# A transformer layer in fp32 split matmuls: single third and fourth tiles at the beginning, modulation passes three steps behind their request, and one multiply moved into the last wait

## The chip, the cores and the metric

The kernel runs on one core of a Trainium2 chip. The metric is the device time of one execution in microseconds. The page of the profile shows one execution, taken with the hardware profiler, on the engines PE (matrix multiply), DVE (vector), ACT (scalar), POOL and SP; PEld is the loading of weights into PE, and SP mostly issues DMA requests.

## The reference

The reference is one layer of a diffusion transformer, followed by a final RMSNorm. There are 256 latent tokens and 256 context tokens, the model width is 2048 (16 tiles of 128), the hidden width of a feed-forward half is 5632 (44 tiles), and everything is float32.

```python
mod_l = (silu_c @ w_mod[l] + b_mod[l]).reshape(B, N_MOD, D_MODEL)      # nine vectors of 2048
mod_c = (silu_cc @ w_mod[l] + b_mod[l]).reshape(1, N_MOD, D_MODEL)
xl = half_step_ffn(xl, mod_l, 0, g_norm[l, 0], w_ffn1_up[l], w_ffn1_down[l])
xc = half_step_ffn(xc, mod_c, 0, g_norm[l, 0], w_ffn1_up[l], w_ffn1_down[l])
hl = adaln(xl, g_norm[l, 1], mod_l, 3)         # rms_norm(x, g) * (1 + mod[i + 1]) + mod[i]
hc = adaln(xc, g_norm[l, 1], mod_c, 3)
...                                            # projections, attention (8 heads), mLSTM (8 heads), w_out
xl = xl + mod_l[:, 5, None, :] * mixer_output(att_l, hm_l, m_l[3], m_gain[l], w_out[l])
xl = half_step_ffn(xl, mod_l, 6, g_norm[l, 2], w_ffn2_up[l], w_ffn2_down[l])
return rms_norm(xl, g_final)
```

A half step is `x + 0.5 * gate * ((silu(a) * b) @ w_down)` with `a, b` the two halves of `adaln(x) @ w_up`. The nine modulation vectors come from a product of one row (two, with the context's) with a matrix of 2048 x 18432.

## The kernel before

**Arithmetic.** Each float32 product is made of three matmuls on parts: a number is split into `hi` (rounded to PE's reduced float32, by ACT, line 128) and `lo` (the remainder, by DVE, line 129), and hi·hi, lo·hi and hi·lo are added in one PSUM bank (`mm3`, line 152). So each weight that arrives by DMA costs ACT one pass, DVE one pass, and PE three matmuls for each block of tokens.

**The beginning.** The first feed-forward needs modulation vectors 0 (shift, `SH`) and 1 (scale, `SC`), which come from the first 32 transfers of 1 MB, `in_w_m`, into four buffers `mraw`. `BLOCKS` says in which order d-model tiles are made ready: tiles 0 and 1 singly, then pairs. For a single tile one transfer gives its shift and one its scale, and `mod_sums` makes both on PE (16 matmuls each, `tr<-mraw,cP`). For a pair four transfers are needed: the shift of its first tile is made by DVE (two passes over the transfer, `junkv<-mraw,cB`, one for each of the two conditions), the shift of its second and the scales of both by PE (16 matmuls of 128 columns, 16 of 256). `mod_turned` then turns the sums into columns (`tr<-ident,row`), x is transposed (`tr<-ident,xs`), scaled, and split into `hhi` and `hlo`. The generator `products` multiplies the tiles that are ready with the first six blocks of columns of the up-projection (weights `raw<-in_w_pre`), in six banks, three matmuls per bank and tile: `mm<-hhi,hi`, `mm<-hhi,lo`, `mm<-hlo,hi`. It gives back control after each bank, and the caller puts one bank's matmuls between two groups of modulation sums, by `steps(prods, n)`. All of this is `Pinned`: PE, DVE and SP work it off in the order in which it is written. `idle(n)` puts n matmuls without a use on PE.

**The mixer.** Vectors 5 to 8 are needed later. Their weights, `in_w_mt`, come as halves of 512 KB into a few slots, and DVE makes one pass (line 208, 128x1024) over each. The class `Beside` hands these passes out: its generator `steps` is called once for each step of the main work, and starts the next pass when the table `PACE` says so and its slot was requested (the transfer is requested a step after the slot's last pass). A step is a weight tile of a projection. The passes' own order on DVE is fixed; between them and the other instructions a scheduler sets the order when the kernel is built. Slots `sr` serve the projections; while the attention and the output projection run, two slots `late` and one or more of `sr` are in use. There DVE also makes the softmax's maximum (line 1683), reciprocal (1688) and scaling (1689, `pr`), which PE transposes (line 1695), and the `lo` parts of `w_out`.

**The end.** `last2` makes the last block of the second feed-forward's down-projection for 256 columns at a time, adds it to the stream (`acc`), and applies the final norm. For the second half of the tokens the last 512 columns come in two halves: DVE adds the first half (line 2348), squares and sums it (2304), multiplies columns 1024 to 1535 by the final gains (`multiplied(1, 2)`, line 2300), adds the second half, squares it, and adds up the sums (2308). POOL makes the power -1/2 of that (2310), and DVE and ACT scale with it (2356, 2358, 2360) and store.

Of the kernel before, what the change touches and what calls it, by code (L numbers as in the profile page):

```python
# [9 lines left out]
F32 = mybir.dt.float32  # L10
# [9 lines left out]
P = 128  # L20
# [13 lines left out]
N_IDLE = 6, 4, 5, 2, 3  # L34
# [10 lines left out]
BLOCKS = ((0, 1), (1, 2)) + tuple((k, k + 2) for k in range(2, 16, 2))  # L45
# [13 lines left out]
def tile_layer(ctx: ExitStack, tc: tile.TileContext, I: dict, out: bass.AP):  # L59
# [207 lines left out]
    class Beside:  # L267
# [5 lines left out]
        def __init__(self, sp, i0, i1, tiles, pace):  # L273
            self.cB = sp.tile([P, 1024], F32, name="cBl", bufs=1)
            self.items = half_items(i0, i1)
            self.pace = pace
            self.slots = {}
# [129 lines left out]
    def products(n_ffn, pre, k0, k1, hhi, hlo, early=False, both=False, middle=False):  # L407
# [26 lines left out]
        for u0 in range(0, 2 * NPRE, most):  # L434
# [3 lines left out]
            if u0 + most < 2 * NPRE and not ahead:  # L438
                ahead.append(load(u0 + most))
            for u in range(nu):  # L440
# [6 lines left out]
                for k, (wh, wl) in ws:  # L447
                    tensor[0].matmul(b, wh, hlo[:, k, :], start=False, stop=k == KT - 1)  # L448
# [13 lines left out]
    with pool(name="st", bufs=1) as st:  # L462
        scratch.append(st)
        cP = st.tile([P, KT, 32], F32, name="cP")
        nc.gpsimd.memset(cP, 0.0)
        pc = tbank()
# [9 lines left out]
        sel = st.tile([96, P], BF16, name="sel")[:, :32]  # L476
        with nc.allow_low_precision("each sum has one term that is not zero, and that is one"):
            vector[0].tensor_reduce(sel, ident[:96, :96].rearrange("p (j q) -> p q j", j=3), axis=AX.X, op=ALU.add)
        c3 = tbank()[:96, :P]
        stack = st.tile([32, P], F32, name="stack")  # L480
        vector[0].tensor_copy(stack[:, :96].rearrange("p (j q) -> p j q", j=3), ident[:32, :32].unsqueeze(1).to_broadcast([32, 3, 32]))
# [78 lines left out]
        def mod_sums(i, k0, k1, last=iter(())):  # L560
# [75 lines left out]
        mod_turned()  # L636
        for s in (CTX, LAT):
            scale_of(0, s, slice(0, 1))
# [10 lines left out]
        for k0, k1 in BLOCKS[1:]:  # L649
            kk = slice(k0, k1)  # L650
            following = products(1, pre, k0, k1, hhi, hlo, middle=True)
            if k1 - k0 == 2:
                raw = mod_unit()
            for i in range(2):
                for _ in mod_sums(i, k0 if i else k1 - 1, k1, following if i else iter(())):
                    steps(prods, 3 - (k1 - k0))
# [7 lines left out]
            if k0 != 2:  # L664
                steps(following)
            mod_turned()
            if k0 != 2:
                steps(prods)
            for s in (CTX, LAT):
                scale_of(0, s, kk)  # L670
            if k0 == 2:
# [13 lines left out]
            if k0 == 2:  # L685
# [1241 lines left out]
    with f2x:  # L1927
# [346 lines left out]
        def last2():  # L2274
# [70 lines left out]
            for h in range(2):  # L2345
# [113 lines left out]
```

## Time and profile before

| | us |
|---|---|
| three runs | 2594.56, 2595.95, 2599.84 (median 2595.95) |
| the profiled execution | 2596.07, of which its span is 2594.4 |
| PE busy | 2565.9 (99%) |
| DVE busy | 2183.9 (84%) |
| ACT busy | 1432.4 (55%) |
| DMA | mean 264 GB/s; 396 GB/s in the first fortieth of the span |

A number on a row of the timeline is the start in microseconds, then the duration, the engine, the line, the operation, output and inputs, shapes, and how often it stands there in a row; in square brackets stands how long the engine had been idle before it, and what ended that. In a table of windows each row is a stretch of time, with the busy microseconds of PE, PEld, DVE, ACT and POOL, each with its count of instructions, then the granted clock of PE (1.00 is full), the share of time in which the DMA engines were busy, and GB/s. PE is busy nearly throughout, so that a change shows in the time only where PE waits (28.5 us in all, 2594.4 less 2565.9), or where its work grows or shrinks.

### The profile page before, as it was taken

The page shows a single profiled execution, that of the slowest core. Times are in us where ns is not written, and L with a number is a line of the kernel's source. Part 1 is how long each engine was busy: PE and PEld are TensorE (multiplying, and loading weights), DVE is VectorE, ACT ScalarE, POOL GpSimd, SP SyncE. Part 2 cuts the span into 40 slices and gives each one's busy share as a digit, 9 for nine tenths or more (in the row PEclk, how much of TensorE's full clock was granted, in tenths as well). Part 3 has the DMA queues.
Part 4 walks back from the last instruction along what each step waited for, and adds up shares of the span by engine and source line. Part 5 has one row for each costly group of instructions (what it writes and reads, how often), then busy time and mean ns, then how long its engine had stood idle before and what let it go on. Part 6 is the DMA issues. An engine that isn't in the chain of part 4 may idle for free. (4 is left out here: it accounts for less than half of the span.)

```text
span 2594.4 us, 34281 instructions
## 1 busy us (share of the span) xinstructions
PE 2565.9 (99%) x12708; PEld 2141.1 (83%) x12708; DVE 2183.9 (84%) x2884; ACT 1432.4 (55%) x1838; POOL 220.5 (8%) x273
## 2 busy tenths in 40 slices
PE   7999999999999999999999999999999999999998
PEld 5788888888888888888889989888898888888887
DVE  6788888878888788888887899798889888888987
ACT  4454444544445565444454448456486676667764
POOL 0000000100000100000110000120000000001001
PEclk9999999999999999999999999999999999999999
DMA  9989999999999989889987897776768999999986
GB/s 396 353 215 266 267 287 273 259 275 287 257 291 264 279 245 244 213 220 224 230 255 258 294 328 239 239 282 212 261 229 251 274 275 277 283 280 284 272 247 174
DMA packets 127656, 684.73 MB, mean 264 GB/s; under 512 B 14200, under 2 KB 16760, under 8 KB 64896
## 3 DMA queue, kind: packets, MB, share of 16 engines
q1 hardware_dynamic: 98112, 490.63, 50.6%
q0 software_dynamic: 29376, 191.90, 37.5%
q8 instruction: 100, 1.64, 0.2%
q14 instruction: 68, 0.56, 0.1%
HBM read 664.59 MB, written 17.89 MB: 263 GB/s over the span
## 5 line engine op out<-in xcount | busy, mean ns | idle before, releaser
L128 ACT ACTIVATE hi<-raw 128x1024 fp32r<-128x1024 f32 (+2 forms) x488 | 505.6, 1040 | 412.6 <-PE mm L152 304.4
L129 DVE TENSOR_TENSOR lo<-raw,hi 128x1024 fp32r<-128x1024 f32 (+2 forms) x476 | 569.0, 1204 | 134.0 <-ACT hi L128 113.2
L128 ACT ACTIVATE hi<-chain 128x1024 fp32r<-128x1024 f32 x352 | 371.9, 1060 | 305.9 <-PE mm L152 184.4
L129 DVE TENSOR_TENSOR lo<-chain,hi 128x1024 fp32r<-128x1024 f32 x352 | 426.5, 1221 | 105.8 <-ACT hi L128 98.3
L152 PE MATMUL mm<-hi,hhi 128*128 128x512 f32 (+3 forms) x1024 | 394.0, 385 | 0.0
L152 PE MATMUL mm<-lo,hhi 128*128 128x512 f32 (+3 forms) x1024 | 386.9, 378 | 0.0
L152 PE MATMUL mm<-hi,hlo 128*128 128x512 f32 (+3 forms) x1024 | 386.4, 377 | 0.0
L208 DVE SCALAR_TENSOR_TENSOR junk<-sraw,cBh 128x1024 fp8e5<-128x1024 f32 x192 | 234.3, 1220 | 21.4 <-DMA sraw<-in_w_mt 19.0
L152 PEld LDWEIGHTS mm<-lo,hhi 128*128 128x128 f32 x1024 | 192.5, 188 | 33.8
L152 PEld LDWEIGHTS mm<-hi,hhi 128*128 128x128 f32 x1024 | 192.6, 188 | 31.1
L152 PEld LDWEIGHTS mm<-hi,hlo 128*128 128x128 f32 x1024 | 192.8, 188 | 30.7
L129 DVE TENSOR_TENSOR lo<-ra,hi 128x1024 fp32r<-128x1024 f32 x104 | 126.3, 1221 | 27.4 <-ACT hi L128 21.6
L128 ACT ACTIVATE hi<-ra 128x1024 fp32r<-128x1024 f32 x104 | 110.2, 1062 | 66.4 <-PE mm L152 40.5
L152 PE MATMUL mm<-lo,hid2h 128*128 128x512 f32 (+1 forms) x356 | 137.9, 387 | 0.1
L152 PE MATMUL mm<-hi,hid2h 128*128 128x512 f32 (+1 forms) x356 | 137.8, 387 | 0.0
L152 PE MATMUL mm<-hi,hid2l 128*128 128x512 f32 (+1 forms) x356 | 137.7, 387 | 0.0
L152 PE MATMUL mm<-hi,sumshl 128*128 128x512 f32 x400 | 123.2, 389 | 0.0
L730 POOL DMA_DIRECT2D chain<-in_w_up1b x60 | 53.1, 886 | 733.5 <-DVE lo L129 733.5
L208 DVE SCALAR_TENSOR_TENSOR sr<-sr,cBl 128x1024 f32<-128x1024 f32 x84 | 102.2, 1224 | 13.4 <-DMA sr<-in_w_mt 7.4
L152 PE MATMUL mm<-hi,sumshh 128*128 128x512 f32 x352 | 108.4, 389 | 0.0
L152 PE MATMUL mm<-hhi,hi 128*128 128x512 f32 (+1 forms) x288 | 101.3, 352 | 0.0
L152 PE MATMUL mm<-hhi,lo 128*128 128x512 f32 (+1 forms) x288 | 99.0, 344 | 0.0
(505 smaller groups left out, 5446.4 us busy)
## 6 DMA issues: line engine op xcount, KB each, us to landing
raw<-in_w_dn SPq DMA_DIRECT2D x70, 1024.0 KB, 9.7
chain<-in_w_up1b POOLq DMA_DIRECT2D x60, 1024.0 KB, 10.6
sraw<-in_w_mt SPq DMA_DIRECT2D x96, 512.0 KB, 8.1
sr<-in_w_mt SPq DMA_DIRECT2D x81, 512.0 KB, 5.6
raw<-in_w_up1b SPq DMA_DIRECT2D x40, 1024.0 KB, 8.0
mraw<-in_w_m SPq DMA_DIRECT2D x32, 1024.0 KB, 8.0
chain<-in_w_dn POOLq DMA_DIRECT2D x30, 1024.0 KB, 9.2
chain<-in_w_up2b POOLq DMA_DIRECT2D x28, 1024.0 KB, 11.2
```

Of the source, the lines that this page charges most:

```text
L128: scalar[0].activation(hi, src, AF.Copy)
L129: vector[0].tensor_tensor(lo, src, hi.bitcast(F32), op=ALU.subtract)
L152: tensor[0].matmul(out_ap, s, m, start=first and not n, stop=last and n == 2, skip_group_check=skip)
L208: ins = nc.vector.scalar_tensor_tensor(junk() if junk else raw, raw, 1.0, cB[s], op0=ALU.mult, op1=ALU.mult, accum_out=mT[:, i, s, kt, h : ...
L730: accum = lambda dst, src: nc.gpsimd.dma_start(dst, src, accum_op=ALU.add)
```

## The change

**The beginning.** `ALONE = 4`: tiles 2 and 3 become single tiles like 0 and 1, and pairs begin at tile 4. Tile 2's shift, which DVE made, is made by PE. A table `AHEAD` says how many banks of the preceding tile's products stand ahead of each group of sums. Four `idle` matmuls stand behind tile 0's turned rows. In single blocks the matmul with `hlo` comes one bank later than those with `hhi`. The transfer of the next products' weights is requested behind the request for modulation weights where it stood ahead of it. Two small tiles, `sel` and `stack`, are made earlier.

On PE, behind the products of the ones of `xs` (x transposed) and tile 0's two groups of sums, there stood (`mm<-hhi,hi` and its two companions are one bank's products; `tr<-mraw,cP` a unit of sums):

```order
L87 MATMUL tr<-mraw,cP 32x128 x16
L87 MATMUL tr<-ident,row 128x128 x2
L87 MATMUL tr<-mraw,cP 32x128 x16
L87 MATMUL mm<-hhi,hi 128x512
L87 MATMUL mm<-hhi,lo 128x512
L87 MATMUL mm<-hlo,hi 128x512
L87 MATMUL mm<-hhi,hi 128x512
L87 MATMUL mm<-hhi,lo 128x512
L87 MATMUL mm<-hlo,hi 128x512
L87 MATMUL tr<-mraw,cP 32x128 x16
```

And now, at the same place:

```order
L92 MATMUL tr<-mraw,cP 32x128 x16
L92 MATMUL tr<-ident,row 128x128 x2
L92 MATMUL mm<-ident 128x128 x4
L92 MATMUL mm<-hhi,hi 128x512
L92 MATMUL mm<-hhi,lo 128x512
L92 MATMUL mm<-hhi,hi 128x512
L92 MATMUL mm<-hhi,lo 128x512
L92 MATMUL mm<-hlo,hi 128x512
L92 MATMUL tr<-mraw,cP 32x128 x16
L92 MATMUL mm<-hhi,hi 128x512
```

Two banks of tile 0's products now come ahead of tile 1's first sums instead of behind them, and the first `hlo` matmul stands behind the second bank's first two. On SP, the order of requests was, from tile 1 on (`raw<-in_w_pre` are the weights of the products):

```order
L557 DMA mraw<-in_w_m 128x2048
L421 DMA raw<-in_w_pre 128x768
L557 DMA mraw<-in_w_m 128x2048 x4
L421 DMA raw<-in_w_pre 128x1536
L557 DMA mraw<-in_w_m 128x2048 x4
L421 DMA raw<-in_w_pre 128x1536
```

It is now:

```order
L566 DMA mraw<-in_w_m 128x2048 x2
L427 DMA raw<-in_w_pre 128x768
L566 DMA mraw<-in_w_m 128x2048 x2
L427 DMA raw<-in_w_pre 128x768
L566 DMA mraw<-in_w_m 128x2048 x2
L427 DMA raw<-in_w_pre 128x768
L566 DMA mraw<-in_w_m 128x2048 x4
L427 DMA raw<-in_w_pre 128x1536
```

The bytes are the same; tiles 2 and 3 have two smaller requests for their products' weights instead of one.

**The mixer.** `LEAD = 3`: a pass starts at the earliest three steps after its transfer was requested. On DVE, in the middle of the second half of the attention (`pr`, `sd` and `nm` belong to the softmax, `yo` and `x_` to the output projection), there stood:

```order
L1688 RECIPROCAL sd<-sd 128x1
L1823 TENSOR_TENSOR x_14449<-x_14449,yo 128x512
L1689 TENSOR_SCALAR pr<-pr,sd 128x512
L208 TENSOR_SCALAR late_14439,mT<-late_14439,cBl 128x1024
L1684 TENSOR_SCALAR nm<-nm 128x1
L129 TENSOR_TENSOR lo<-raw,hi 128x1024
L1688 RECIPROCAL sd<-sd 128x1
L208 TENSOR_SCALAR late_14439,mT<-late_14439,cBl 128x1024
L1689 TENSOR_SCALAR pr<-pr,sd 128x512
```

And now:

```order
L1702 RECIPROCAL sd<-sd 128x1
L1837 TENSOR_TENSOR x_14501<-x_14501,yo 128x512
L1703 TENSOR_SCALAR pr<-pr,sd 128x512
L213 TENSOR_SCALAR late_14492,mT<-late_14492,cBl 128x1024 x2
L213 TENSOR_SCALAR late_14493,mT<-late_14493,cBl 128x1024
L1697 TENSOR_REDUCE nm<-mm 128x1
L1836 TENSOR_TENSOR yo<-mm,gate 128x512
L1698 TENSOR_SCALAR nm<-nm 128x1
L134 TENSOR_TENSOR lo<-raw,hi 128x1024
L1702 RECIPROCAL sd<-sd 128x1
L1837 TENSOR_TENSOR x_14502<-x_14502,yo 128x512
L1703 TENSOR_SCALAR pr<-pr,sd 128x512
```

No pass stands between `sd` and `pr` now; three stand together behind a `pr`. Such a group of three `late` passes comes three times, and 12 passes instead of 8 follow the softmax's last `pr`.

**The end.** `multiplied(1, 2)` moves behind the last `factor`. DVE's last instructions were (`L2300` is the multiply):

```order
L2348 TENSOR_TENSOR acc_16127<-acc_16127,mm 128x256
L2304 TENSOR_SCALAR sab,rstd<-acc_16127 128x256
L2300 TENSOR_TENSOR acc_16127<-acc_16127,gf 128x512
L2348 TENSOR_TENSOR acc_16127<-acc_16127,mm 128x256
L2304 TENSOR_SCALAR sab,rstd<-acc_16127 128x256
L2308 TENSOR_REDUCE s_21134<-rstd 128x1
L2358 TENSOR_SCALAR acc_16127<-acc_16127,rstd 128x512
```

They are now:

```order
L2362 TENSOR_TENSOR acc_16185<-acc_16185,mm 128x256
L2318 TENSOR_SCALAR sab,rstd<-acc_16185 128x256
L2362 TENSOR_TENSOR acc_16185<-acc_16185,mm 128x256
L2318 TENSOR_SCALAR sab,rstd<-acc_16185 128x256
L2322 TENSOR_REDUCE s_21191<-rstd 128x1
L2314 TENSOR_TENSOR acc_16185<-acc_16185,gf 128x512
L2371 TENSOR_SCALAR acc_16185<-acc_16185,rstd 128x512
```

The multiply stands between the sum `s` and the scaling that waits for POOL.

The diff, cut to its core:

```diff
+LEAD = 3
-N_IDLE = 6, 4, 5, 2, 3
+N_IDLE = 6, 4, 5, 2, 3, 4
+AHEAD = {1: (2, 2, 1), 2: (0, 1, 2), 3: (0, 1, 2), 4: (1, 2, 2, 1)}
-BLOCKS = ((0, 1), (1, 2)) + tuple((k, k + 2) for k in range(2, 16, 2))
+ALONE = 4
+BLOCKS = tuple((k, k + 1) for k in range(ALONE)) + tuple((k, k + 2) for k in range(ALONE, 16, 2))
...
             pin(queue.dma_start(x, I["w_mt"][i - 2, kt, :, h * 1024 : (h + 1) * 1024]))
             self.slots[self.asked] = x, limit
+            self.since[self.asked] = self.done
...
-                    if self.n not in self.slots or self.done < np.interp(self.n, *zip((0, 0), *self.pace)) + self.waits:
+                    if self.n not in self.slots or self.done < max(np.interp(self.n, *zip((0, 0), *self.pace)) + self.waits, self.since[self.n] + LEAD):
                         break
...
+            behind = []
             for u in range(nu):
...
-                for k, (wh, wl) in ws:
-                    tensor[0].matmul(b, wh, hlo[:, k, :], start=False, stop=k == KT - 1)
+                behind += [(b, k, wh) for k, (wh, wl) in ws]
+                while behind and (k1 - k0 > 1 or u == nu - 1 or len(behind) > 1):
+                    o, k, wh = behind.pop(0)
+                    tensor[0].matmul(o, wh, hlo[:, k, :], start=False, stop=k == KT - 1)
                 yield
...
-                if g == KT // nk - 1:
+                if g == KT // nk - 1 and k1 > ALONE + 2:
                     steps(last)
                 raw = mod_unit()
+                if g == KT // nk - 1 and k1 <= ALONE + 2:
+                    steps(last)
...
         mod_turned()
+        idle(N_IDLE[5])
...
+            ahead = iter(AHEAD.get(k0, ()))
+            steps(prods, next(ahead, 0))
             for i in range(2):
                 for _ in mod_sums(i, k0 if i else k1 - 1, k1, following if i else iter(())):
-                    steps(prods, 3 - (k1 - k0))
+                    steps(prods, next(ahead, 3 - (k1 - k0)))
...
-                if not h:
-                    multiplied(1, 2)
             r = factor(sss[1][:, :6])
+            multiplied(1, 2)
```

What is left out makes `sel` and `stack` ahead of the first transpose, and puts `ALONE` where the loop over the blocks had 2.

More of the change, by code (lines that the diff above doesn't have):

```diff
@@ L276, in __init__ @@
             self.pace = pace
-            self.slots = {}
+            self.slots, self.since = {}, {}
             self.n = self.done = self.waits = self.asked = 0
@@ L465, in tile_layer @@
         nc.gpsimd.memset(cP, 0.0)
+        stack = st.tile([32, P], F32, name="stack")
+        pin(nc.vector.tensor_copy(stack[:, :96].rearrange("p (j q) -> p j q", j=3), ident[:32, :32].unsqueeze(1).to_broadcast([32, 3, 32])))
+        sel = st.tile([96, P], BF16, name="sel")[:, :32]
+        with nc.allow_low_precision("each sum has one term that is not zero, and that is one"):
+            pin(nc.vector.tensor_reduce(sel, ident[:96, :96].rearrange("p (j q) -> p q j", j=3), axis=AX.X, op=ALU.add))
         pc = tbank()
@@ L662, in tile_layer @@
                     biased(0, k0, k0 + 1)
-            if k0 != 2:
+            if k0 != ALONE:
                 steps(following)
             mod_turned()
-            if k0 != 2:
+            if k0 != ALONE:
                 steps(prods)
@@ L670, in tile_layer @@
                 scale_of(0, s, kk)
-            if k0 == 2:
+            if k0 == ALONE:
                 steps(following)
```

7 lines of the change are left out of this document (1 added, 6 removed).

## The prediction

> **What bounds the kernel now.** I read the page first, then PE's waits and a table of windows over the beginning, the timeline of PE, SP and DVE there, then the same views where the mixer's passes run, and the end of the timeline.
>
> ```profile
> PE 2565.9 (99%) x12708; PEld 2141.1 (83%) x12708; DVE 2183.9 (84%) x2884; ACT 1432.4 (55%) x1838; POOL 220.5 (8%) x273
> ```
>
> PE is the bound. Of the span of 2594.4 us it is idle 28.5 us, and no part of the change takes work from PE, so what can be gained lies inside these 28.5 us. Nothing near the 0.2% that a measurement of this kernel can tell from no change (5.2 us) comes easily. PE's waits of the first 60 us:
>
> ```profile
> PE tr L87 <- DMA mraw<-in_w_m: 5.8, 3, 3.0
> PE tr L467 <- ACT cc L191: 2.9, 1, 2.9
> PE mm L87 <- DVE thirds L87: 1.5, 1, 1.5
> ```
>
> and the windows there:
>
> ```profile
> 20.00:25.00 5.00, 1.89 (x35) 1.36 (x35) 3.06 (x10) 4.48 (x8) 0.00 (x0) 0.97 1.01 419
> 25.00:30.00 5.00, 5.00 (x43) 3.53 (x43) 0.32 (x1) 1.07 (x4) 0.00 (x0) 0.69 1.00 421
> 30.00:35.00 5.00, 4.50 (x49) 2.99 (x47) 3.08 (x11) 1.82 (x5) 0.00 (x0) 1.00 1.02 424
> 55.00:60.00 5.00, 5.00 (x54) 3.97 (x53) 2.62 (x5) 2.92 (x7) 0.00 (x0) 1.00 1.02 428
> 60.00:65.00 5.00, 5.00 (x45) 2.75 (x44) 4.93 (x6) 1.67 (x3) 0.00 (x0) 1.00 0.92 329
> ```
>
> Until 60 us the DMA engines are busy all the time at about 420 GB/s; in 20 to 25 us PE works 1.89 of 5.00. From 55 us on PE has no gap, and in 60 to 65 us the transfers fall to 0.92, since buffers are not yet free. So the beginning is bound by the transfers up to some point near 60 us, and by PE behind it. Only what PE has still to do at that point counts.
>
> **Part one, the beginning.** The rows that bear on it, from the timeline of PE and DVE:
>
> ```profile
> 23.61 1.08 PE L87 MATMUL tr<-mraw,cP 128*32 128x128 f32 x32 [2.98 <-DMA mraw<-in_w_m]
> 36.82 2.29 DVE L87 SCALAR_TENSOR_TENSOR junkv<-mraw,cB 128x2048 fp8e5<-128x2048 f32 x1
> 38.58 1.07 PE L87 MATMUL tr<-mraw,cP 128*32 128x256 f32 x16 [1.54 <-DMA mraw<-in_w_m]
> 50.83 1.07 PE L87 MATMUL tr<-mraw,cP 128*32 128x256 f32 x16 [1.25 <-DMA mraw<-in_w_m]
> 55.06 1.04 PE L87 MATMUL tr<-ident,xs 128*128 128x128 f32 x8
> 55.86 0.48 PE L87 MATMUL mm<-hhi,hi 128*128 128x512 f32 x1
> 56.17 0.39 PE L87 MATMUL mm<-hhi,lo 128*128 128x512 f32 x1
> 56.40 0.40 PE L87 MATMUL mm<-hhi,hi 128*128 128x512 f32 x1
> 58.78 1.08 PE L87 MATMUL tr<-mraw,cP 128*32 128x128 f32 x32
> 63.98 1.07 PE L87 MATMUL tr<-mraw,cP 128*32 128x256 f32 x16
> ```
>
> A unit of sums takes PE 1.08 us. The pairs' units at 38.58 and 50.83 still wait for their transfer, those at 58.78 and 63.98 no longer. The unit at 63.98 is the last of tiles 6 and 7. How long its data had been there is told by its transfer, the second of the two requests in this answer on `mraw`, of which the later took the longer to land:
>
> ```profile
> L557 SPq DMA_DIRECT2D mraw<-in_w_m x2: 328/328/328, 50.8 to 52.0; - x2
> DMA to landing us min/median/max: 7.3/8.8/10.4
> ```
>
> It was requested at 52.0 and landed 10.4 us later, at 62.4. The bytes ahead of it are the same after the change (tiles 2 and 3 need four units of 1 MB and 768 KB of product weights, whether as a pair or singly), and the DMA engines have no free time ahead of it, so it cannot land earlier. From this unit on the order on PE is as before. The gain is therefore at most 63.98 - 62.4 = 1.6 us.
>
> What costs: for the pair 2, 3 PE made three units, for two single tiles it makes four, so one unit more, 1.08 us; four dummies at the pace of the eight matmuls of 128 columns between 55.06 and 55.86, 0.1 us each, 0.4 us. Both lie ahead of 45 us, where PE waits longer than that for transfers (2.98 and 1.54 us in the rows, then 1.25), so their price is nothing while these waits last, and 1.5 us if they were gone. The `hlo` matmuls that come a bank later, and the products that come ahead of the sums, are the same in number. On DVE the change takes away two passes of 2.29 us, work that hardly counted, as DVE is busy for 2.62 of 5.00 us in 55 to 60 us. SP's reordered requests stand one unit later: 1 MB at 420 GB/s is 2.5 us, and the weights of the products have a whole block for it.
>
> What gains: tile 2's products may start when tile 2 alone is scaled and no longer when both are. A pair has twelve triples of products, each of about 3 x 0.23 = 0.7 us (from 56.17 to 56.40); singly, tile 2's six, 4.1 us, are there to be run in the waits of 1.54 and 1.25 us, 2.8 us together. That is more than the cap of 1.6 us. I take 1.4, near the cap, and leave 0.2 for the seams between groups. Ends: -1.6 (the cap) and +1.5 (the waits gone, the extra work exposed).
>
> The clock of PE is the weak point. The rows, in windows of 3.41 us:
>
> ```profile
> 21.26:24.68 3.42, 1.07 (x33) 0.90 (x33) 2.22 (x5) 3.15 (x4) 0.00 (x0) 1.00 1.02 424
> 24.68:28.09 3.41, 3.41 (x21) 2.35 (x22) 0.00 (x0) 0.28 (x1) 0.00 (x0) 0.50 1.01 425
> ```
>
> After a window with 1.07 us of work the granted clock is 0.50 for a whole one. In it 21 matmuls took 3.41 us, and at the full clock the same would take half, so that 1.7 us are lost, all of it within the stretch bound by transfers. The dummies and the two early banks put about 0.4 + 5 x 0.23 = 1.5 us of work ahead of tile 1's sums, and may bring that window's share up far enough or not. [...] The sum does not change by it: a lost 1.7 us would come back out of waits that the transfers set, and only the cap counts.
>
> **Part two, the passes in the mixer.** The windows, and the waits of PE and DVE in 1640 to 1870 us:
>
> ```profile
> 1800.00:1835.00 35.00, 33.41 (x196) 28.07 (x195) 29.57 (x59) 18.98 (x35) 0.00 (x0) 1.00 0.68 232
> 1835.00:1870.00 35.00, 35.00 (x156) 28.98 (x155) 30.12 (x41) 14.38 (x15) 0.00 (x0) 1.00 0.76 258
> 1870.00:1900.00 30.00, 30.00 (x158) 25.08 (x157) 27.35 (x43) 22.04 (x44) 0.00 (x0) 1.00 0.58 183
> ```
> ```profile
> DVE late L208 <- DMA late<-in_w_mt: 1.6, 1, 1.6
> PE tr L1695 <- DVE pr L1689: 2.0, 2, 1.6
> PE tr L1606 <- DVE SH L213: 0.4, 1, 0.4
> ```
>
> The place of that wait, from the timeline:
>
> ```profile
> 1829.67 1.23 DVE L208 SCALAR_TENSOR_TENSOR late<-late,cBl 128x1024 f32<-128x1024 f32 x1 [1.58 <-DMA late<-in_w_mt]
> 1830.82 0.48 DVE L1689 TENSOR_SCALAR pr<-pr,sd 128x512 f32<-128x512 f32 x1
> 1831.44 0.63 PE L1695 MATMUL tr<-ident,pr 128*128 128x128 f32 x4 [1.58 <-DVE pr L1689]
> 1834.12 1.23 DVE L129 TENSOR_TENSOR lo<-raw,hi 128x1024 fp32r<-128x1024 f32 x1 [1.69 <-PE mm L1704]
> ```
>
> A pass in front of the softmax's `pr` waits 1.58 us for its transfer, and PE then waits 1.58 us for `pr`. With three steps between request and pass, the order has no pass there. This pass is gone from the place, and PE's 1.58 us with it. The remaining 0.4 (the other `pr`) and 0.4 (`SH`) come to at most 2.4 us altogether; I count 1.6. What is late next is the weights' `lo` parts, which DVE makes ahead of PE: at 1834.12 DVE itself waits 1.69 us for PE.
> What it costs: no pass is added, but three of them at 1.15 us, 3.45 us together, stand behind one `pr`, and four more than before fall behind the last `pr`. Four are 4.6 us; in 1835 to 1900 us DVE has 65.00 - 57.47 = 7.5 us free, so they fit. A group of 3.45 us hides behind about 1.15 us of PE's slack at that place (the pass and its wait took 2.73 us, PE lost 1.58) and behind DVE's lead of about 1.7 us: 2.85 of 3.45, which leaves 0.6 us if it hits. Ends: -2.4, and +10.4 with three groups in full view. Before and behind these places nothing changes that PE waits for; moved passes earlier in the mixer run beside windows of PE that are full.
>
> **Part three, the end.**
>
> ```profile
> 2585.80 0.68 DVE L2300 TENSOR_TENSOR acc<-acc,gf 128x512 f32<-128x512 f32 x1
> 2586.41 0.41 DVE L2348 TENSOR_TENSOR acc<-acc,mm 128x256 f32<-128x256 f32 x1
> 2587.32 0.16 DVE L2308 TENSOR_REDUCE s<-rstd 128x1 f32<-128x6 f32 x1
> 2587.62 0.55 POOL L2310 TENSOR_TENSOR rstd<-s,mhalf 128x1 f32<-128x1 f32 x1 [5.69 <-DVE s L2308]
> 2588.21 0.49 DVE L2358 TENSOR_SCALAR acc<-acc,rstd 128x512 f32<-128x512 f32 x1 [0.73 <-POOL rstd L2310]
> 2585.28 0.28 PE L152 MATMUL mm<-lo,hid2h 128*128 128x256 f32 x1
> ```
>
> The last matmul starts at 2585.28, so the bank for the second half is full by 2585.6, while DVE multiplies from 2585.80 to 2586.41. Without the multiply the second add, the sum, POOL's power and the scaling come 2586.41 - 2585.80 = 0.6 us earlier. The multiply then lies in DVE's wait of 0.73 us for POOL, and takes 0.68: it just fits. Ends: -0.6 and 0 (the wait is filled to 0.05 us, and the delayed scaling gives the rest back). I take -0.6, as both rows agree on it.
>
> **Sum.** -1.4 - 1.6 - 0.6 = -3.6 us on the profiled 2596.07, which is 0.1 above the median of the three runs: 2592.5 us, 0.14% faster and inside what counts as the same.
>
> **Rivals.** *The beginning gives nothing.* If tile 3's sums and the extra unit eat what the waits gave, or the clock falls to 0.50 at another place nearer to 60 us, the term is 0 or up to +1.5. Time 2596.07 - 1.6 - 0.6 = 2593.9 to 2595.4. For it: the row at half clock, and the cap of only 1.6. Against: waits of 1.54 and 1.25 us directly in the path.
> *The groups of passes stall PE.* Three groups of 3.45 us with only PE's slack of 1.15 to hide them are 2.3 each, 6.9 us, and with nothing hidden 10.4; on 2596.07 - 1.4 - 0.6 that is 2601.0 to 2604.5. It decides from 1.2 us for each group on, where 3 x 1.2 eats the 3.6. For it: the row at 1831.44, where one late pass cost 1.58. Against: a group comes behind `pr`, not ahead of it, and PE needs the next `pr` steps later.
> *Everything to its cap.* -1.6 - 2.4 - 0.6 = -4.6: 2591.5. To be faster by over 0.2% something else of the 28.5 us must fall as well.
> *The change does nothing at its places.* The wait moves to another transfer in part two (term 0): 2594.1.
>
> **Chances.** The forecast with its neighbours from 2591 to 2593.5: 0.45; nothing at the beginning: 0.20; the wait only moved: 0.10; groups that stall, 0.15, of which 0.12 end over 2601.1 and 0.03 below; everything to the cap 0.10, and over 0.2% faster in nearly all of that only if a run comes out 0.7 us lower, for which I give the whole 0.10 since the three runs spread by 5 us. So faster 0.10, same 0.78, slower 0.12. The range leaves out the stalled groups and the lower tail: 2590.0 to 2598.5, the upper end being the sum with +1.5 at the beginning and +1.5 for one group partly in view.
>
> **What would show it.** Right: the unit that stood at 63.98 starts near 62.5, PE's waits for `mraw` fall from 5.8 us, and the total of idle time falls by 3 to 4 us; no PE wait on `pr` above 0.5 us; `L2308`'s sum 0.6 us nearer to PE's last matmul. Wrong: a clock of 0.50 behind 45 us, PE waits on `pr`, `SH` or `lo` behind a group of three passes, a scaling that starts later than POOL's end. The prediction fails if PE's busy time grows by over 1.5 us, or if the other order of passes makes a wait in a stretch of the mixer where PE has none now.

## The result

The changed kernel took 2605.77 us (median of 11 executions, 2598.19 to 2609.49) against 2596.34 us of the kernel before (11, 2594.16 to 2604.02). The ratio is 1.0034, with a 95% interval of 1.0026 to 1.0041: slower by 6.7 to 10.6 us. A second comparison, in the experiments below, gave 1.0021 (1.0009 to 1.0033). Of the executions of all runs one, of the spacing alone, took 12917 us; it is left out of that run's ratio, and its cause is not known. Forecast were 2592.5 us, with a range up to 2598.5.

The page of the changed kernel's profile (the line of helper `split` is 133 and 134 here, the passes' line is 213):

```profile
span 2602.2 us, 34437 instructions
PE 2572.4 (99%) x12781; PEld 2147.8 (83%) x12781; DVE 2179.3 (84%) x2887; ACT 1433.8 (55%) x1842; POOL 218.4 (8%) x273
```

The span grew by 7.8 us, from 2594.4, and so did PE's busy time, by 6.5. PE was given about 2.1 us of work: the unit of sums, 1.08, and the four dummies, which the trace has as eight matmuls:

```profile
20.22 1.06 PE L92 MATMUL mm<-ident 128*128 128x128 f32 x8
```

Most of the rest is the same work at a lower clock: ahead of the end the changed kernel's profile has three stretches of 3.41 us at a granted clock of 0.50 (from 57.56, 1491.16 and 1883.69 us), that of the kernel before one (from 24.68), and a unit of sums that took 1.08 us at full clock counts as 1.93 us of busy time at 57.54. So the idle time in the page (29.8 us, before 28.5) hides most of what happened; the windows with their granted clock show it.

Two stretches hold what was lost. Worked out from the traces, by matching each matmul with the same one of the kernel before, PE's work of 1400 to 1600 us took 4.2 us longer and that of 1860 to 1930 us 3.9 (of each, 2.1 idle and about 2 more busy time at a lower clock). The second stretch, in windows of 5 us, and then two windows of the kernel before:

```profile
1875.00:1880.00 5.00, 4.62 (x21) 3.50 (x19) 5.00 (x10) 2.12 (x3) 0.00 (x0) 1.00 0.86 339
1880.00:1885.00 5.00, 2.59 (x10) 2.09 (x11) 4.96 (x11) 1.04 (x1) 0.00 (x0) 0.87 0.20 64
1885.00:1890.00 5.00, 5.00 (x23) 4.04 (x22) 3.49 (x5) 2.80 (x7) 0.00 (x0) 0.79 0.98 351
```
```profile
1875.00:1880.00 5.00, 5.00 (x25) 3.88 (x24) 4.50 (x7) 2.82 (x5) 0.00 (x0) 1.00 0.74 242
1880.00:1885.00 5.00, 5.00 (x27) 4.17 (x26) 3.76 (x6) 5.00 (x10) 0.00 (x0) 1.00 0.83 251
```

PE idles for 2.4 us in 1880 to 1885, and the clock is 0.87 and then 0.79. In the kernel before PE is busy and the clock is 1.00. Rows of the timeline there, on DVE, ACT and PE (`gv` is the column of gate values that is made from the passes' sums of one modulation vector; PE turns it):

```profile
1877.32 1.22 DVE L213 SCALAR_TENSOR_TENSOR sr<-sr,cBl 128x1024 f32<-128x1024 f32 x1
1877.43 0.24 ACT L1872 ACTIVATE h2hi<-SH 128x32 fp32r<-128x32 f32 x1 [3.73 <-DVE late L213]
1878.47 1.28 DVE L1836 TENSOR_TENSOR yo<-mm,gate 128x512 f32<-128x512 f32 x2
1879.67 1.28 DVE L1837 TENSOR_TENSOR x<-x,yo 128x512 f32<-128x512 f32 x2
1880.87 0.17 DVE L218 TENSOR_TENSOR gv<-mT 128x16 f32<-128x16 f32 x1
1881.06 1.21 DVE L134 TENSOR_TENSOR lo<-raw,hi 128x1024 fp32r<-128x1024 f32 x1
1882.19 0.16 DVE L219 TENSOR_TENSOR gv<-gv,vecs 128x16 f32<-128x16 f32 x1
1882.41 0.28 PE L362 MATMUL tr<-ident,gv 128*16 128x128 f32 x1 [2.78 <-DVE gv L219]
```

The last pass (1877.32) is done at 1878.5. Then come the output projection's additions, the two small instructions that make `gv`, a weight's `lo` between them, and PE has waited 2.78 us for the result. ACT, too, stands 3.73 us behind a small instruction that waits for the last pass but one, with weights to split behind it. In the kernel before there stood:

```profile
1863.38 1.22 DVE L208 SCALAR_TENSOR_TENSOR late<-late,cBl 128x1024 f32<-128x1024 f32 x1
1864.64 0.17 DVE L213 TENSOR_TENSOR gv<-mT 128x16 f32<-128x16 f32 x1
1864.85 0.18 DVE L214 TENSOR_TENSOR gv<-gv,vecs 128x16 f32<-128x16 f32 x1
1872.05 0.27 PE L356 MATMUL tr<-ident,gv 128*16 128x128 f32 x1
```

There `gv` was ready at 1865.03, 7 us before PE turned it, and nothing stood between the last pass and `gv`. In the changed kernel PE reached the turn at 1882.41 - 2.78 = 1879.63, about 1.1 us behind the end of the last pass; the additions (2.4 us) and the `lo` (1.2 us) that now stand ahead of the last `gv` are together longer than the wait. So two things came together: the late pass used up most of the 7 us, and the order on DVE puts work between it and `gv`. No run takes the two apart.

PE's longest waits of the changed kernel in 1400 to 2010 us:

```profile
PE tr L362 <- DVE gv L219: 2.8, 1, 2.8
PE tr L1436 <- ACT cy L1474: 2.1, 1, 2.1
```

The wait for the softmax's `pr` is gone from this list. The second wait (1488 us) was not in the kernel before, and it stands in the other of the two stretches. The second profile of the changed kernel, below, has no such wait; over all profiles of this text it lies between 0 and 2.1 us.

The beginning, first one window of the kernel before, then windows of the changed kernel and its units of sums on PE:

```profile
50.00:55.00 5.00, 4.17 (x31) 3.02 (x32) 3.46 (x11) 0.39 (x1) 0.00 (x0) 1.00 1.02 429
```
```profile
50.00:55.00 5.00, 4.50 (x36) 2.77 (x34) 2.90 (x11) 2.68 (x5) 0.00 (x0) 1.00 0.88 320
55.00:60.00 5.00, 2.46 (x34) 2.02 (x35) 4.93 (x7) 2.28 (x6) 0.00 (x0) 0.76 1.01 427
60.00:65.00 5.00, 5.00 (x44) 2.98 (x42) 4.73 (x7) 1.58 (x2) 0.00 (x0) 0.90 1.01 419
```
```profile
57.54 1.93 PE L92 MATMUL tr<-mraw,cP 128*32 128x128 f32 x32 [2.99 <-DMA mraw<-in_w_m]
64.28 1.07 PE L92 MATMUL tr<-mraw,cP 128*32 128x256 f32 x16
```

In 50 to 55 us the transfers are at 0.88 and 320 GB/s, where they had been at 1.02 and 429. PE then waits 2.99 us for a unit, works it at half speed (1.93 us instead of 1.08), and the unit that had started at 63.98 starts at 64.28. One of SP's waits in 28 to 58 us tells why the transfers paused:

```profile
SPq L566 <- DVE SH L92: 4.1, 1, 4.1
```

The request for tile 7's shift stood 4.1 us behind the buffer that DVE was emptying with its two passes (46.44 to 51.06). It was made at 51.1 us; in the kernel before, where another buffer was taken for it, at 48.05. DVE's two passes had begun at 46.12 there, so they are hardly later now; it is the turn of the buffers that changed.

The end:

```profile
2594.58 0.16 DVE L2322 TENSOR_REDUCE s<-rstd 128x1 f32<-128x6 f32 x1
2594.66 0.68 DVE L2314 TENSOR_TENSOR acc<-acc,gf 128x512 f32<-128x512 f32 x1
2594.88 0.86 POOL L2324 TENSOR_TENSOR rstd<-s,mhalf 128x1 f32<-128x1 f32 x1 [5.15 <-DVE s L2322]
2595.78 0.49 DVE L2371 TENSOR_SCALAR acc<-acc,rstd 128x512 f32<-128x512 f32 x1 [0.44 <-POOL rstd L2324]
```

POOL's power takes 0.86 us where it had taken 0.55. From the sum to the scaling are 1.2 us, before 0.9.

### The profile page after: what moved, and what is told of

Same layout as the page of the kernel before. It is cut to its first block, busy times and chain, and to the rows that moved or that the text cites. A ratio compares the mean times of both kernels' runs of the same rounds, so it can differ in the third digit from the quotient of the medians.

```text
span 2602.2 us, 34437 instructions
## 1 busy us (share of the span) xinstructions
PE 2572.4 (99%) x12781; PEld 2147.8 (83%) x12781; DVE 2179.3 (84%) x2887; ACT 1433.8 (55%) x1842; POOL 218.4 (8%) x273
## 5 line engine op out<-in xcount | busy, mean ns | idle before, releaser
L133 ACT ACTIVATE hi<-raw 128x1024 fp32r<-128x1024 f32 (+3 forms) x486 | 504.0, 1041 | 424.8 <-PE mm L157 319.0
L157 PE MATMUL mm<-hlo,hi 128*128 128x512 f32 (+1 forms) x288 | 99.1, 344 | 0.0
```

The lines of the kernel that those rows point to most:

```text
L133: scalar[0].activation(hi, src, AF.Copy)
L157: tensor[0].matmul(out_ap, s, m, start=first and not n, stop=last and n == 2, skip_group_check=skip)
```

## The experiments

My theory after these traces: the spacing makes the last pass late, the gate's column with it, and PE pays for the wait twice, once idle and once at a lower clock. The new beginning gains nothing because of the order in which buffers are handed out. Against it stood that the waits at 1488 and 1882 us need both the beginning and the spacing, or were a chance of that execution. Each figure such as 1.0019 is the ratio of a kernel's time to that of the kernel before on the same chip, with its 95% interval, from 11 or 12 executions against 27 to 35.

**One part alone.** The first runs each had one of the three parts: the new beginning (`LEAD = 0`, the multiply at its old place), the spacing (the three lines of `Beside` in the diff above and `LEAD = 3`), the multiply (its move alone).

> The kernel before with the new beginning alone: no spacing of the passes, the multiply at its old place. The theory of the places: the beginning brings nothing, because the transfer for tile 7's shift waits for the buffer that DVE holds, PE then waits about 3 us at 57 us and runs at half clock behind it; the first matmul behind 1400 us comes 0 to 1.5 us later than before, and the time is +0 to +2 us. The rival, that the beginning gains as I forecast and the profile of the changed kernel fell on a bad execution: -1 to -2 us.

> The kernel before with the spacing of three steps alone. The theory that the spacing carries the whole loss: +6.5 to +9 us, with the same two waits of PE, 2 to 3 us for the convolution's columns near 1488 us and 2.5 to 3 us for the gate's column near 1880 us, and a window at half clock behind each. The rival, that the waits come out of the new beginning's shift and the spacing meet together: under +3 us, and one of the two waits missing.

> The kernel before with the multiply in the last wait alone. By my forecast -0.6 us, and DVE's wait for POOL's power falls from 0.73 us to under 0.2; by the other end 0, when the scaling starts later behind the multiply.

Measured: the beginning 1.0003 (0.9992 to 1.0013), the spacing 1.0019 (1.0007 to 1.0030), the multiply 1.0000 (0.9990 to 1.0010). The spacing alone made the kernel slower by 1.8 to 7.8 us. The wait and the half clock near 57 us came in the beginning alone as expected, but behind 1400 us its matmuls start 3.3 us later, not 0 to 1.5; where that comes from is taken up below. PE's longest waits of the spacing alone in 1640 to 1900 us, and its windows:

```profile
PE tr L359 <- DVE gv L216: 3.6, 1, 3.6
PE tr L1527 <- DVE den L1531: 0.6, 1, 0.6
```
```profile
1875.00:1880.00 5.00, 1.48 (x7) 0.90 (x5) 5.00 (x13) 2.13 (x3) 0.00 (x0) 0.92 0.56 221
1880.00:1885.00 5.00, 4.95 (x13) 3.89 (x14) 3.98 (x7) 1.71 (x3) 0.00 (x0) 0.50 0.60 187
```

The wait for `gv` is there, 3.6 us, and the clock is 0.50 behind it: 13 matmuls in 5 us where there were 27 in the kernel before. The wait at 1488 us is not there, though the order of instructions there is the same. So half of my expectation fell. The multiply's gain, by the trace, is in the part on the end below; its time cannot be told from nothing.

**Which buffer is taken.** The new beginning alone, with the same instructions in the same order on PE, DVE and SP, and four single buffers instead of a pool of four, so that the buffer which DVE empties is taken third:

```diff
-        unit = iter(range(32))
+        unit = iter(zip(range(32), [0, 1, 2, 3] * 3 + [1, 2, 0, 3, 2, 0, 1, 3, 0, 1, 2, 3] * 2))
...
-            raw = st.tile([P, 2048], F32, tag="mraw", name="mraw", bufs=4)
+            n, place = next(unit); raw = st.tile([P, 2048], F32, tag=f"mraw{place}", name="mraw", bufs=1)
...
```

> The new beginning alone, with the same instructions in the same order, but the buffers of the modulation weights handed out otherwise from tile 6 on: the buffer that DVE empties is taken third and not second. The theory of the places: the transfers no longer pause, PE's wait near 57 us falls from 3.0 to under 1.5 us and the unit that ends tiles 6 and 7's sums starts 1 to 2 us earlier than in the new beginning alone; time 1 to 3 us below that of the new beginning alone. The rival, that the transfers themselves set that time: no difference over 0.5 us.

Measured 1.0005 (0.9995 to 1.0015): the gain of 1 to 3 us that I expected against the beginning alone (1.0003) does not show in the time. In the trace a change does: SP's wait for DVE, and two of PE's units, are

```profile
SPq L566 <- DVE SH L92: 1.5, 1, 1.5
```
```profile
56.36 1.08 PE L92 MATMUL tr<-mraw,cP 128*32 128x128 f32 x32 [1.96 <-DMA mraw<-in_w_m]
63.04 1.07 PE L92 MATMUL tr<-mraw,cP 128*32 128x256 f32 x16 [1.41 <-DMA mraw<-in_w_m]
```

The last unit starts at 63.04, 1.3 us ahead of the beginning alone (64.37) and 0.9 ahead of the kernel before. PE's first wait is 1.96 us, not under 1.5 as I expected, and a second one of 1.41 stands where the pause has moved. The rival, no difference over 0.5 us, fell: the order of the buffers moves that unit, and what it then waits for is its transfer.

**Which passes.** The changed kernel again, and the kernel before with the spacing for the first 100 passes, for the last 28, and for the first 116:

```diff
-... self.since[self.n] + LEAD):
+... self.since[self.n] + (LEAD if self.n < 100 else 0)):
```

with `>= 100` and `< 116` in the other two.

> The changed kernel once more, as the yardstick for the other three. If the loss is of the program: +6 to +10 us over the kernel before, with PE's wait for the gate's column near 1880 us at 2.5 to 3.6 us. If it was of the executions or the chip: under +3 us.

> The kernel before with the spacing of three steps for the first 100 of the 128 passes only; the last 28 go as before. The theory that the loss sits in the last passes: -1 to +1 us, no wait for the gate's column, the wait for the softmax's scaling near 1830 us as before (0.8 to 1.6 us). The theory that the wait for the convolution's columns near 1488 us, seen in the changed kernel's profile, is a loss of the spacing: +3 to +4 us.

> The spacing for the last 28 passes only. The theory that the loss sits in the last passes: +4 to +6 us, with a wait of 2.5 to 3.6 us for the gate's column and a stretch at half clock behind it, less 1.5 us for the softmax's scaling. The rival, that it sits in the first hundred: -1 to -2 us.

> The spacing for the first 116 passes, the last 12 without it, so that no pass stands between the softmax's last sums and its scaling but one, and the last pass stands ahead of the gate's column as before. If the lateness of the last pass is the whole loss: -2 to 0 us, no wait for the gate's column, and the wait for the softmax's scaling under 0.8 us. If the groups of passes themselves stall PE: +2 us or more.

Measured: the changed kernel 1.0021 (1.0009 to 1.0033), the first 100 passes 1.0008 (0.9998 to 1.0018), the last 28 passes 1.0013 (1.0002 to 1.0023), the first 116 passes 0.9996 (0.9986 to 1.0006). The changed kernel was 2.3 to 8.6 us slower, a little less than I had expected of it. PE's wait for `gv` in the changed kernel's second profile and in that of the last 28 passes:

```profile
PE tr L362 <- DVE gv L219: 1.9, 1, 1.9
```
```profile
PE tr L359 <- DVE gv L216: 2.7, 1, 2.7
```

In the runs of the first 100 and the first 116 passes there is none. With the first 116 spaced, PE's longest wait there is

```profile
PE mm L154 <- DVE lo L131: 1.3, 2, 0.9
```

and none for `pr`. So the last 12 passes decide: with the spacing the last of them ends only 0.3 to 2.0 us before PE reaches the turn of `gv`, in the four profiles that have it, and PE waits for what DVE still does in between; without it `gv` is ready 7.0 us ahead, with `LEAD = 2` (below) 4.8. The groups of three before them don't stall PE at the softmax. The 1.3 us for `lo`, near 1703 and 1710 us, are not in the kernel before, and the run of the first 100 passes has 1.2 of them: they are a cost of that spacing. Its ratio, 1.0008, fits neither of the two theories named for it better than the other.

**The mends together.** The changed kernel with the spacing up to pass 116, and the same with the buffers' order; the kernel before with `LEAD = 2` for all passes.

> The changed kernel with the last 12 passes free of the spacing, all else as changed. If the late last passes are the whole loss: -1 to +1.5 us to the kernel before (the beginning +0.5, the softmax's wait -1.5, the end -0.3), and no wait of PE for the gate's column. If another part of the change costs something that the single runs did not show: +3 us or more.

> The same, with the buffers of the modulation weights handed out as in the run on the buffers. If both mends add up: -1 to -3 us to the kernel before, and 1 to 1.5 us under the run without the buffers' order, which is about what 12 executions can tell. The unit that ends tiles 6 and 7's sums starts at about 63.0 us and no longer at 64.3 to 64.7.

> The kernel before with a spacing of two steps for all passes. In the order of its instructions the last pass and the gate's column stand where they stood before, and a pass stands ahead of the softmax's last scalings again. If the place of the last pass decides, and not the spacing as such: -1.5 to +1.5 us, no wait for the gate's column. If any spacing starves the last passes: +3 us or more.

Measured: 1.0016 (1.0008 to 1.0025), 1.0009 (1.0000 to 1.0018), and 1.0005 (0.9996 to 1.0014). The first two missed my expectation. In both the wait for `gv` is gone from the profile, and in the second the unit that ends tiles 6 and 7's sums starts at 63.08 as expected; yet the first is 2 to 6.5 us slower than the kernel before, and the second 0 to 4.7. With `LEAD = 2` no loss can be measured, as the place of the last pass told; the softmax's wait is at 0.4 us:

```profile
PE tr L1698 <- DVE pr L1692: 0.4, 1, 0.4
```

**Who carries the rest.** The beginning alone and the mended changed kernel a second time, beside the mended one without the new beginning (spacing to pass 116 and the multiply's move on the kernel before), and `LEAD = 2` with the multiply's move.

> The new beginning alone, a second time. Open is whether it costs anything in the mean over executions: its profiles stand 0.4 us behind the kernel before at 100 us. If that is all: 0 to +1 us. If it costs more than its profiles show, as the changed kernel with the last passes mended (+4 us) suggests: +2 to +4 us.

> The changed kernel with the last 12 passes free, a second time. If +4 us was chance: 0 to +2 us. If the beginning and the spacing of the first passes together cost more than each: +3 to +5 us.

> The same without the new beginning. If the beginning carries those 4 us: -1 to +0.5 us, 2 us or more under the run beside it. If it does not: within 1.5 us of the run beside it.

> The kernel before with a spacing of two steps and the multiply in the last wait. The two by their traces: the softmax's wait near 1830 us -1.5, the end -0.25: -2 to 0 us, which 12 executions can hardly tell from nothing.

Measured: 1.0014 (1.0005 to 1.0024), 1.0020 (1.0010 to 1.0029), 1.0002 (0.9993 to 1.0011), 0.9999 (0.9989 to 1.0009). With the new beginning the mended kernel is slower twice, without it it is not, and the beginning alone is slower in the second of its two comparisons, while the first (1.0003) cannot be told from 1. So the beginning carries about 0.1 to 0.2%, by three of its four comparisons. No version beats the kernel before by what can be measured.

Where it carries it is another matter. The following is worked out from the traces: how much later the same matmuls start than in the profile of the kernel before, in us, as the median over the matmuls of a stretch (columns: the start of the stretch).

```
                                       100-140  900-940 1000-1200 1620-1680 1720-1760 1845-1870 1930-1980
changed                                   0.4      0.8       0.6       4.8       5.1       3.3       7.3
changed, second profile                   0.7      0.4       0.1       0.5       2.4       0.7       2.1
beginning alone                           0.4      0.1       3.2       4.6       5.9       5.4       4.6
beginning alone, second                  -0.7     -0.7       3.6       5.8       6.8       5.1       5.0
changed, spacing to 116                   0.0     -0.3       2.1       3.4       4.8       3.1       2.1
changed, spacing to 116, second          -0.2     -0.2       3.7       5.1       6.6       4.8       4.0
beginning alone, buffers' order          -1.0     -1.2      -1.5      -1.1      -0.6      -2.0      -2.9
spacing alone                             0.4      0.6       0.3       0.7       1.9       0.2       6.1
last 28 passes                            0.4      0.4       0.1       0.8       1.2      -0.7       3.4
first 116 passes                          0.8      0.5       0.3       1.1       2.8       1.0       1.4
first 116, multiply                       0.1      0.1      -0.1       0.5       2.9       1.1       1.7
multiply alone                            0.2      0.8       4.6       5.4       6.5       5.6       5.2
```

From the sixth column to the seventh the kernels with late last passes lose 1.4 to 5.9 us. From the fifth to the sixth those with the spacing there gain 1.7 to 1.8, the last 28 passes 1.9. The others gain 0.5 to 1.7 there without it, since their waits for `pr` are 0.5 to 1.5 us long, by execution, where the profile of the kernel before has 2.0; so of the 1.8 only 0.1 to 1.3 are the spacing's. But at 100 us the new beginning stands between -0.7 and +0.7, and the profiles of ten kernels with the old one spread from -0.8 to +1.3. The loss of the beginning isn't at the beginning. (The rows are of single executions, and not all are typical: the two profiles of the beginning alone are the slowest of its 12 and 11 executions, and that of the buffers' order is the fastest of its 12.)

Between the second and third columns some profiles jump by 2 to 4 us, at 940 to 955 us, in work that no part of the change touches. There ACT waits for a buffer `stg` whose store is late. The timeline of ACT and the windows behind it, of the kernel before, and then of the second run of the beginning alone:

```profile
944.26 0.60 ACT L833 ACTIVATE stg<-tr 128x512 f32<-128x512 f32 x1 [0.88 <-DMA hid<-stg]
```
```profile
950.00:955.00 5.00, 5.00 (x23) 4.13 (x22) 5.00 (x7) 4.42 (x6) 0.00 (x0) 1.00 0.34 141
955.00:960.00 5.00, 5.00 (x23) 3.92 (x22) 5.00 (x6) 2.12 (x2) 0.00 (x0) 1.00 0.86 293
```
```profile
946.51 0.60 ACT L847 ACTIVATE stg<-tr 128x512 f32<-128x512 f32 x1 [3.54 <-DMA hid<-stg]
```
```profile
950.00:955.00 5.00, 3.75 (x17) 2.75 (x15) 5.00 (x6) 5.00 (x7) 0.00 (x0) 1.00 0.61 210
955.00:960.00 5.00, 4.36 (x12) 3.46 (x13) 4.77 (x6) 1.65 (x2) 0.00 (x0) 0.66 0.47 143
```

The store took 5.3 us in the one and 8.2 in the other; ACT's wait grows from 0.88 to 3.54, PE waits 1.9 us, and the clock falls to 0.66. This jump stands in four of the six profiles with the new beginning and the pool's own order of buffers, and in two of the twelve others. In these six the store landed after 7.4 to 9.1 us, in the twelve without the jump after 4.4 to 5.3. That is how 2 to 4 us could come and go with so little change at the start, but six and twelve profiles don't prove that the beginning makes it more frequent. A second `stg` buffer would be the test; no run has one. So it stays open by which way the beginning costs its 0.1 to 0.2%.

**The power at the end.** The kernel before, with columns 1024 to 1535 multiplied by the gains and the factor in one instruction, and so without the multiply that was moved:

```diff
-                if not h:
-                    multiplied(1, 2)
...
-                if cb == 3:
-                    pin(nc.vector.scalar_tensor_tensor(a, a, r, gf(3), op0=ALU.mult, op1=ALU.mult))
+                if cb in (2, 3):
+                    pin(nc.vector.scalar_tensor_tensor(a, a, r, gf(cb), op0=ALU.mult, op1=ALU.mult))
```

> The kernel before without the multiply in the last wait or ahead of it: columns 1024 to 1535 are multiplied by the gains and by the factor in one instruction at the end, as columns 1536 to 2047 are. The theory that POOL's power is slower while DVE multiplies beside it (0.3 us more from the sum to the scaling in the run of the multiply alone): from the sum to the scaling 0.9 us as before, not 1.2, and the sum 0.55 us nearer to the last matmul. The rival, that the sum itself is what became slower: 1.2 us here too.

One execution each, the multiply alone and then this kernel:

```profile
2592.88 0.16 DVE L2308 TENSOR_REDUCE s<-rstd 128x1 f32<-128x6 f32 x1
2592.95 0.68 DVE L2300 TENSOR_TENSOR acc<-acc,gf 128x512 f32<-128x512 f32 x1
2593.18 0.86 POOL L2310 TENSOR_TENSOR rstd<-s,mhalf 128x1 f32<-128x1 f32 x1 [5.15 <-DVE s L2308]
2594.08 0.49 DVE L2357 TENSOR_SCALAR acc<-acc,rstd 128x512 f32<-128x512 f32 x1 [0.44 <-POOL rstd L2310]
```
```profile
2588.44 0.16 DVE L2308 TENSOR_REDUCE s<-rstd 128x1 f32<-128x6 f32 x1
2588.74 0.55 POOL L2310 TENSOR_TENSOR rstd<-s,mhalf 128x1 f32<-128x1 f32 x1 [5.15 <-DVE s L2308]
2589.33 1.41 DVE L2354 SCALAR_TENSOR_TENSOR acc<-acc,rstd,gf 128x512 f32<-128x512 f32 x2 [0.73 <-POOL rstd L2310]
```

With nothing beside it the power takes 0.55 us and the scaling follows the sum by 0.89; with the multiply beside it 0.86 and 1.20. In the eight profiles with the multiply moved the power takes 0.86, in the ten others 0.55. The theory holds. The second part of the expectation missed: the sum starts 1.87 us behind the start of the last matmul, against 2.04 in the kernel before, so 0.17 nearer and not 0.55. In the rows the multiply still had 0.45 us to go when POOL began, and POOL took 0.31 more (0.86 less 0.55); what holds POOL up there, no run shows.

## Why the prediction was wrong

**The sum** was -3.6 us and the measured change +6.7 to +10.6. The forecast named slower than 0.2% with 0.12.

**Part two, the passes.** The step that failed is "Four are 4.6 us; in 1835 to 1900 us DVE has 65.00 - 57.47 = 7.5 us free, so they fit", and with it "nothing changes that PE waits for". It asked whether DVE has room for the passes, and not by when the last one must be done. A spacing behind the request, with a few slots that are requested again only after their pass, limits the number of passes per step: the transfers come three at a time, and the passes too. The last pass started 14 us later (1863.38, then 1877.32), of which 3.3 are the lag of the whole kernel at that point; that used up most of the 7 us by which `gv` had been ready early, the column became the last thing that PE waited for, and the term was +1.4 to +5.9 us where 0 was taken. The order before and after showed that more passes follow the softmax, and the next reader of their sums, and what DVE does between the last pass and that reader, were not looked up. The rival of stalling groups had the right sign and the wrong place: the groups at the softmax hide, as the run to pass 116 shows.

**The softmax's wait** was right in its mechanism: there is no wait for `pr` in the kernels with the spacing there. Its size, -1.6, was read from one execution with a long wait. Against that profile the spaced kernels gain 1.7 to 1.9 us between 1720 and 1870 us, but unspaced ones gain 0.5 to 1.7 too.

**The earlier passes** were taken at nothing. The lists show waits for `lo` and `den` near 1705 us in the kernels with the first passes spaced (1.3 us in the run to pass 116, 1.0 in that of the spacing alone, `den` 0.6 of it), against the statement that they run beside full windows. That statement was read from windows in which PE is full only as long as DVE is on time.

**Part one, the beginning.** The step that failed is to take 62.4 us as the landing time after the change too, since the bytes are the same and "the DMA engines have no free time ahead of it", with the 1.4 us that were taken next to its cap. The cap of 1.6 holds as a cap, but a transfer also needs a buffer. The buffers came round in another order, SP's next request stood behind the one that DVE emptied from 46.44 to 51.06, and the transfer that had landed at 62.34 landed at 64.09. With another buffer taken, 0.9 us of the 1.6 were there. In place of -1.4 its own place shows 0 (-0.7 to +0.7), and the time 0.1 to 0.2% more, of which the way is open. The four dummies cost about 1 us and not 0.4, which hid in PE's waits. The stretch at half clock, which begins between 22 and 39 us in all ten profiles with the old beginning, is in none of the eight with the new one, and as forecast this gave nothing at 100 us (-0.7 to +0.7).

**Part three, the end.** "It just fits" failed in its size: from the first of DVE's two last additions to the sum are 1.79 us in the run of the multiply alone where they were 2.32, about the 0.6 of the forecast, but POOL's power is 0.31 us longer beside the multiply, so that 0.2 is left at the scaling. From the start of the last matmul to the end of the span nothing of it is seen: 8.95 to 9.50 us in the eight profiles with the move, 9.07 to 9.40 in the nine with the multiply at its old place. That end of the range (0) was named, with another cause.

**What was left out of the terms of part two** is the clock behind a wait. Each wait was priced at its length. A wait of 3.6 us cost 5.9, since 5 us at a clock of 0.50 followed. One of 1.9 left the clock at 1.00 in all windows of 1870 to 1890 us of the changed kernel's second profile, and one of 1.9 near 955 us was followed by 0.66. The traces show a pattern. In the 16 profiles with two or more stretches at 0.50 all of a profile begin on one grid of 3.41 us, which lay differently against the work from profile to profile (counted from the span's start, it begins at 0.78 us in the kernel before's and at 2.94 in the changed kernel's). Of some 13,500 stretches of these grids at full clock, in all 18 profiles, between the first record of the clock (at 11.02 us in the kernel before, 9.77 in the changed kernel) and the last matmuls, the 18 in which PE was busy for 1.53 us or less were all followed by half clock; of the eleven with 1.55 to 1.87 us two were; of those with more, none. The beginning alone shows it at one and the same wait, the 1.9 us near 955 us: in its first profile 1.98 us of work were left in the stretch, and the clock stayed; in its second 1.52, and it fell.

## What to carry to other kernels

When work is put off on an engine with time to spare, ask who reads the last of it and what the engine does between the two, not only whether it has room: the chain behind the last item is what moves. A row of full DMA windows is no proof that transfers cannot start earlier or later; look also at what the requests wait for, buffer by buffer, since a request that stands behind one busy buffer holds up those behind it: here SP stood 4.1 us for the buffer that DVE was emptying; that request went out at 51.1 us and the one behind it at 51.5, though PE was done with a unit's buffer at 49.35. And where PE is 99% busy, price a new wait with the clock behind it: in these traces a wait that took 1.9 us or more out of one stretch of 3.41 us was followed by a stretch at 0.50 each time, one that took less than 1.5 never. Half of that stretch, 1.7 us, is an estimate of what it costs on top; behind the wait of 3.6 us it was 2.3 (5.9 less 3.6).

## What the runs showed of the hardware that I had not expected

A power of one column on POOL took 0.55 us alone and 0.86 beside a multiply of two operands on DVE.

In each of the 16 profiles with two or more stretches of PE at half clock, these began on one grid of 3.41 us. Between the first record of the clock and the last matmuls, a stretch at full clock in which PE was busy for 1.53 us or less was followed by half clock in all 18 cases, one with more than 1.87 in none. The matmuls at half clock count as busy: in the changed kernel's profile PE's busy time grew by 6.5 us with about 2.1 us of work added.

The same instruction order gave profiles that differ by up to 4 us in stretches which no part of the change touches. One store of 256 KB landed after 4.4 to 5.3 us in twelve profiles and after 7.4 to 9.1 in six, and with one buffer behind it those six lost 2 to 4 us there. Over 27 to 35 executions the kernel before spread by some 10 to 13 us, so that 12 executions tell about 0.1%.
